# Second layer of a two-layer trunk: attention output projection by token halves, with the split weights of six units kept for the second half

## The chip, the cores and the metric

The kernel runs on one core of a Trainium2 chip. The metric is the time of one execution on the device in microseconds (us); the median of several runs counts.

## The reference

512 latent tokens and 256 context tokens of width 1024 pass two layers, each a token mixer and a squared-ReLU MLP. Every sub-layer sits between two RMS norms, modulated by a conditioning vector. The second layer's mixer is a neighbourhood attention; only its latent tokens are needed. After the attention this is what the second layer computes:

```python
def rmsnorm(t, g):
    tf = t.astype(jnp.float32)
    tf = tf * lax.rsqrt(jnp.mean(tf * tf, axis=-1, keepdims=True) + RMS_EPS)
    return tf.astype(t.dtype) * g

def sq_relu_mlp(h, w1, w2):
    return jnp.square(jax.nn.relu(h @ w1)) @ w2

def finish_layer(t, y, m, g, w1, w2):
    t = t + m[2] * rmsnorm(y, g[1])
    h2 = modulate(rmsnorm(t, g[2]), m[3], m[4])
    return t + m[5] * rmsnorm(sq_relu_mlp(h2, w1, w2), g[3])
...
            y = neighbourhood_attention(h, kc, vc, na_w_qkv[j], na_rpb[j]) @ na_w_out[j]
...
        x = finish_layer(x, y, m_lat, g, mlp_w1[i], mlp_w2[i])
```

`na_w_out` is 1024 x 1024, `w1` 1024 x 4096, `w2` 4096 x 1024, all in float32.

## The kernel before

Channels lie on the 128 partitions in eight blocks (`KB`), tokens along the free dimension: 512 latent tokens (`LAT`), for the first layer 256 context tokens more. The products are made in three passes of a reduced format: each operand is split into a high part (a copy in that format) and a low part (the rest), and high x high, high x low and low x high are added up in PSUM.

Weights come as units of 128 x 1024 (all eight input blocks for one block of 128 output channels). `Units.next` (L132) takes a unit that `wload` (L105) has loaded into one of two `raw` buffers (every third one into a third buffer, `raw2`), and `wsplit` (L114) splits it: ScalarE (ACT) writes the high part `wh` (L119), VectorE (DVE) the low part `wl` (L120), into two tiles each that take turns. TensorE (PE) then makes 24 matmuls per unit and column range, in `mm3` (L144).

The second layer's part after the attention is this. ACT copies the last attention result of a head pair out of PSUM (L1141), DVE adds the two halves (L1142, L1143); after all pairs each block is split into high and low (L1213, L1214). The output projection (L1235 to L1243) takes eight units against all 512 tokens, in two accumulators that take turns. After each unit `sums.add` (L295) works on the result: ACT squares it (L299) and scales it into the residual branch (L389), which frees the accumulator, DVE multiplies it by the stream x (L305), ACT squares the scaled one (L306), and GpSimd (POOL) adds the three products to running sums (L309). After the last unit `sums.factors` (L311) makes the norm factors of a token: PE adds the sums over the partitions (row sums, L263), DVE and ACT work out a reciprocal root (L321, L246 to L250), PE spreads it over the partitions again (L274) and ACT copies it (L275); the factors of the next norm (L334 to L338) follow in the same way. `join` (L361) goes over the eight blocks: multiply by the factor and add to x (`add_block`, L351 and L352: blocks 2, 4, 6 on POOL, the others on DVE), then split the modulated result into high (ACT, L377) and low (DVE, L378). This feeds the MLP (`mlp`, L884): four chunks, of each eight hidden units (`hidden`, L902) and then the product with `w2` (L954), added up by DVE (L960). The first two hidden units are begun together, block by block, as the blocks come out of the join; the list `early` says over which tokens, in which order. The last chunk's product (`c == 3`) goes by halves of 256 tokens (`HALVES`); each half loads and splits the eight units. After each half `after1` makes the factors of the last norm, adds and stores.

The order on each engine is made at build time by a scheduler from the program's order; `wsplit` runs under a higher priority (L117), so that splits are placed early on ACT and DVE. An engine works its list strictly in that order.

## Time and profile before

| what | us |
|---|---|
| median of 3 runs | 2187.4 |
| lowest, highest run | 2185.53, 2195.42 |
| profiled execution | 2191.73 |
| its span | 2189.9 |
| PE busy | 2073.0 (95% of the span) |
| DVE, ACT, POOL busy | 1278.6 (58%), 1008.4 (46%), 514.3 (23%) |
| mean granted clock of PE | 0.975 |

The profiled execution took 4.3 us more than the median. Times in the trace count from the start of the span. A PE row's duration includes its pipeline, so that the distance of two starts (the pitch) tells what a matmul costs. The granted clock is a share of 2.4 GHz.

### The profile page before, as it was taken

Reading aid. Unit: us, or ns where it says so; the run is one execution under the profiler, and the core shown is the slowest. Engines: PE = TensorE matmul, PEld = TensorE weight load, DVE = VectorE, ACT = ScalarE, POOL = GpSimd, SP = SyncE. Lnnn points to the kernel's source line nnn. Section 1 sums busy time; section 2 is a strip of 40 time slices with the busy share of each in tenths; the row PEclk is TensorE's granted clock in tenths of the full one; section 3 lists DMA queues with packets and bytes.
Section 4 is the critical chain, followed back from the end, with each engine's and each line's share of the span. In section 5 each row is a group of like instructions: output and inputs, shape, how many; then the busy total and the mean of one; then the engine's idle time right before and its main releaser. Section 6 shows DMA issues by size and latency. Waiting matters only on the chain.

```text
span 2189.9 us, 32496 instructions
## 1 busy us (share of the span) xinstructions
PE 2073.0 (95%) x12848; PEld 1733.5 (79%) x12848; DVE 1278.6 (58%) x2023; ACT 1008.4 (46%) x1751; POOL 514.3 (23%) x486
## 2 busy tenths in 40 slices
PE   6999998999999888999999999889999989999996
PEld 3777876878878766888888888668898768889895
DVE  5657968576683687314334244488777664345356
ACT  4565756567473553213223133356556643323244
POOL 0004435254451462000000001633222260000004
PEclk8999999999999999999999999989999989999998
DMA  6446758357676422333333111321111114222233
GB/s 253 135 152 187 234 158 238 115 173 221 192 200 235 156 74 85 107 114 116 116 116 114 59 59 68 106 78 50 56 54 54 49 50 155 95 97 87 97 107 115
DMA packets 93868, 269.72 MB, mean 123 GB/s; under 512 B 13074, under 2 KB 21652, under 8 KB 93716
## 3 DMA queue, kind: packets, MB, share of 16 engines
q1 hardware_dynamic: 85268, 242.47, 34.0%
q0 software_dynamic: 8448, 25.18, 4.4%
q8 instruction: 101, 1.65, 0.3%
q14 instruction: 51, 0.42, 0.1%
HBM read 244.27 MB, written 23.33 MB: 122 GB/s over the span
## 4 chain that ended last, share of the span: by engine, by line
PE 79%; DVE 9%; ACT 4%; DMA 3%; issue 2%; POOL 2%; SPq 0%; DVEq 0%; ACTq 0%; POOLq 0%
PE acc L902 21%; PE acc L144 21%; PE acc L954 20%; PE a L1048 4%; DMA E<-crow 2%; PE s L169 2%; PE a L1059 2%; PE yp L1134 1%; PE s L629 1%; DVE wl L120 1%; PE s L708 1%; PE pt L1119 1%; PE s L724 1%; PE s L263 1%; ACT wh L119 1%
## 5 line engine op out<-in xcount | busy, mean ns | idle before, releaser
L119 ACT ACTIVATE wh<-raw 128x1024 fp32r<-128x1024 f32 (+1 forms) x241 | 254.2, 1055 | 686.7 <-PE acc L954 309.7
L120 DVE TENSOR_TENSOR wl<-raw,wh 128x1024 fp32r<-128x1024 f32 (+1 forms) x241 | 301.9, 1253 | 255.1 <-ACT wh L119 248.6
L144 PE MATMUL acc<-hh,wh 128*128 128x512 f32 (+1 forms) x976 | 286.2, 370 | 7.8 <-ACT wh L119 3.0
L144 PE MATMUL acc<-hl,wh 128*128 128x512 f32 (+1 forms) x976 | 264.1, 346 | 0.5 <-DVE hl L762 0.5
L144 PE MATMUL acc<-hh,wl 128*128 128x512 f32 (+1 forms) x976 | 262.6, 344 | 2.0 <-DVE wl L120 2.0
L902 PE MATMUL acc<-hh,wh 128*128 128x258 f32 (+2 forms) x1024 | 242.8, 317 | 9.5 <-ACT hh L377 9.5
L954 PE MATMUL acc<-ah,wh 128*128 128x512 f32 (+1 forms) x832 | 247.4, 347 | 4.1 <-DVE ya L960 4.0
L902 PE MATMUL acc<-hl,wh 128*128 128x258 f32 (+2 forms) x1024 | 241.8, 314 | 3.9 <-DVE hl L378 3.8
L954 PE MATMUL acc<-ah,wl 128*128 128x512 f32 (+1 forms) x832 | 244.5, 343 | 0.8 <-DVE wl L120 0.8
L954 PE MATMUL acc<-al,wh 128*128 128x512 f32 (+1 forms) x832 | 244.8, 344 | 0.0
L902 PE MATMUL acc<-hh,wl 128*128 128x258 f32 (+2 forms) x1024 | 240.8, 313 | 0.0
L144 PEld LDWEIGHTS acc<-hh,wh 128*128 128x128 f32 (+1 forms) x976 | 155.2, 190 | 60.9 <-issue 38.3
L902 PEld LDWEIGHTS acc<-hh,wh 128*128 128x128 f32 x1024 | 160.9, 191 | 33.5 <-issue 11.5
L309 POOL TENSOR_TENSOR syy<-syy,last 128x512 f32<-128x512 f32 (+2 forms) x24 | 38.3, 1596 | 585.6 <-ACT last L299 585.5
L144 PEld LDWEIGHTS acc<-hh,wl 128*128 128x128 f32 (+1 forms) x976 | 153.7, 190 | 27.5 <-DVE wl L120 2.5
L902 PEld LDWEIGHTS acc<-hl,wh 128*128 128x128 f32 x1024 | 161.2, 191 | 17.9 <-DVE hl L378 5.9
L144 PEld LDWEIGHTS acc<-hl,wh 128*128 128x128 f32 (+1 forms) x976 | 154.2, 190 | 25.3 <-DVE hl L762 1.1
L902 PEld LDWEIGHTS acc<-hh,wl 128*128 128x128 f32 x1024 | 161.8, 191 | 11.6 <-DVE wl L120 0.4
L954 PEld LDWEIGHTS acc<-ah,wh 128*128 128x128 f32 x832 | 139.4, 189 | 32.7 <-issue 13.1
L954 PEld LDWEIGHTS acc<-ah,wl 128*128 128x128 f32 x832 | 139.6, 189 | 21.9 <-DVE wl L120 1.0
L954 PEld LDWEIGHTS acc<-al,wh 128*128 128x128 f32 x832 | 139.5, 189 | 20.0
L960 DVE TENSOR_TENSOR ya<-ya,acc 128x768 f32<-128x768 f32 (+2 forms) x56 | 40.6, 726 | 196.1 <-PE acc L954 196.1
(320 smaller groups left out, 3813.0 us busy)
## 6 DMA issues: line engine op xcount, KB each, us to landing
raw<-in_w_dram SPq DMA_DIRECT2D x136, 512.0 KB, 3.4
mraw<-in_modw_dram SPq DMA_DIRECT2D x72, 512.0 KB, 3.3
raw<-in_win_dram SPq DMA_DIRECT2D x48, 512.0 KB, 4.0
E<-crow SPq DMA_DIRECT2D x96, 256.0 KB, 5.0
eb<-erow POOLq DMA_DIRECT2D x96, 128.0 KB, 5.5
raw<-in_wout_dram SPq DMA_DIRECT2D x24, 512.0 KB, 3.7
raw<-in_modw_dram SPq DMA_DIRECT2D x8, 1024.0 KB, 17.8
raw<-in_wqk_dram SPq DMA_DIRECT2D x16, 512.0 KB, 3.3
```

The lines of the kernel that those rows point to most:

```text
L119: act.activation(wh[:, :n], raw[:, :n], AF.Copy)
L120: dve.tensor_tensor(wl[:, :n], raw[:, :n], wh[:, :n].bitcast(F32), ALU.subtract)
L144: pe.matmul(acc[:m, s0:s1], lhsT=ww[:, i * m:(i + 1) * m], rhs=xx[:, k, s0:s1], start=first and i == 0 and j == 0, stop=last and i == len( ...
L169: mm = pe.matmul(ps[32 * j:32 * j + 32, hf * 256:hf * 256 + 256], lhsT=cact[:, 8 * kg + 2 * j:8 * kg + 2 * j + 32], rhs=raw[:, j * 256:j * ...
L263: pe.matmul(ps[32 * j:32 * j + 32], lhsT=ones[:, :32], rhs=t[i], start=i == 0, stop=i == len(t) - 1)
L309: pool.tensor_tensor(t[:, s0:s1], t[:, s0:s1], d, ALU.add)
L629: pe.matmul(ps, lhsT=btok[:, d, c], rhs=xw.rearrange("p e q -> p (e q)"), start=True, stop=True)
L902: pe.matmul(acc[:, d0:d0 + s1 - s0], lhsT=ww[wi], rhs=xx[:, k, s0:s1], start=k == 0 and j == 0, stop=k == KB - 1 and j == 2)
L954: pe.matmul(acc[:, s0:s1], lhsT=ww[:, k * P:(k + 1) * P], rhs=xx[:, s0:s1], start=k == 0 and j == 0, stop=k == KB - 1 and j == 2)
L960: dve.tensor_tensor(y, y, acc[:, p0:p1], ALU.add)
L1048: pe.matmul(acc[:, :s1 - s0], lhsT=ws[ww][:, k * P:(k + 1) * P], rhs=xx[:, k, s0:s1], start=k == 0 and j == 0, stop=k == KB - 1 and j == 2)
L1059: pe.matmul(acc, lhsT=xx[:, k, i * P:(i + 1) * P], rhs=w[ww][:, sl], start=k == 0 and n == 0, stop=k == KB - 1 and n == 2)
```

## The change

In the second layer the projection now runs over the two token halves one after the other. In the first half the units 2 to 7 are split into tiles of their own (12 of 128 x 1024, in a pool that is opened when the attention's pool is closed and takes its place), and the second half uses them again; units 0 and 1 are loaded and split again. Norm factors and `join` come after each half. The MLP's first two units take the first half's tokens for all blocks, and then those of the second. In the last pass of the MLP's product, the units 2 to 7 are split in the first half into `hh` and `hl`, which nothing needs any more, and are used again in the second: six loads and six splits fewer.

```diff
--- before.py
+++ after.py
@@ -112,7 +112,16 @@
         sp.dma_start(raw[:, :src.shape[-1]], src)
         return raw
 
-    def wsplit(raw, n=1024):
+    def wsplit(raw, n=1024, into=None):
+        if into:
+
+            wh, wl = into
+            if len(wh.shape) == 3:
+                raw = raw.rearrange("p (k c) -> p k c", k=KB)
+            with tc.high_priority():
+                act.activation(wh, raw, AF.Copy)
+                dve.tensor_tensor(wl, raw, wh.bitcast(F32), ALU.subtract)
+            return into
         wh = wpool.tile([P, 1024], F32R, tag="wh", name="wh", bufs=2)
         wl = wpool.tile([P, 1024], F32R, tag="wl", name="wl", bufs=2)
         with tc.high_priority():
@@ -129,11 +138,11 @@
         def prefetch(self):
             self.ahead.append(wload(self.src[self.n + len(self.ahead)]))
 
-        def next(self):
+        def next(self, into=None):
             if not self.ahead:
                 self.prefetch()
             self.n += 1
-            return wsplit(self.ahead.pop(0))
+            return wsplit(self.ahead.pop(0), into=into)
 
     def mm3(acc, w, xh, xl, segs, first=True, last=True, m=P, ks=range(KB)):
         wh, wl = w
@@ -942,16 +951,23 @@
                     next(pieces, None)
                 for i, part in enumerate(passes if c == 3 else [(0, n)]):
                     w2.n = c * KB
+                    keep = c == 3 and len(passes) == 2 and l == 1
                     segs = [(max(part[0], s0), min(part[1], s1)) for s0, s1 in seg if s0 < part[1] and s1 > part[0]]
                     p0, p1 = part
                     for o in range(KB):
                         acc = acc_tile()
-                        wh, wl = w2.next()
+
+                        into = [q[:, :, (o - 2) * P:(o - 1) * P] for q in (hh, hl)] if keep and o > 1 else None
+                        if into and i:
+                            ww_ = into
+                        else:
+                            ww_ = [q if len(q.shape) == 3 else q.rearrange("p (k c) -> p k c", k=KB) for q in w2.next(into)]
+                        wh, wl = ww_
                         for k in range(KB):
                             ah, al = hid[k]
                             for j, (ww, xx) in enumerate(((wh, ah), (wh, al), (wl, ah))):
                                 for s0, s1 in segs:
-                                    pe.matmul(acc[:, s0:s1], lhsT=ww[:, k * P:(k + 1) * P], rhs=xx[:, s0:s1],
+                                    pe.matmul(acc[:, s0:s1], lhsT=ww[:, k], rhs=xx[:, s0:s1],
                                               start=k == 0 and j == 0, stop=k == KB - 1 and j == 2)
                         y = res[:, o, p0:p1]
                         if c == 0:
@@ -1232,15 +1248,22 @@
     A6 = scaled("A6", 1, 2, 4, True)
     hh, hl = yh, yl
     shift_cols(1, 3, LAT, hh, hl)
-    for p0, p1 in SEG[:1]:
-        wno = Units(a["wno"])
-        for o in range(KB):
-            acc = acc_tile()
-            mm3(acc, wno.next(), yh, yl, [(p0, p1)])
-            sums.add(o, acc, y1, x2, G5, p0, p1)
-        sl = slice(p0, p1)
-        sums.factors((0, 1))
-        join(y1, x2, sums, sl, A6, 0, hh, hl)
+
+    wno = Units(a["wno"])
+    with tc.tile_pool(name="wr", bufs=1) as wr:
+        parts = []
+        for n, (p0, p1) in enumerate(HALVES):
+            for o in range(KB):
+                acc = acc_tile()
+                if n == 0 and o > 1:
+                    parts.append(wno.next([wr.tile([P, 1024], F32R, name=f"w{q}{o}") for q in "hl"]))
+                elif n and o == 0:
+                    wno.n = 0
+                mm3(acc, parts[o - 2] if o > 1 else wno.next(), yh, yl, [(p0, p1)])
+                sums.add(o, acc, y1, x2, G5, p0, p1)
+            sl = slice(p0, p1)
+            sums.factors((n,))
+            join(y1, x2, sums, sl, A6, 0, hh, hl)
 
 
     G7 = [None]
@@ -1259,7 +1282,7 @@
                 sp.dma_start(out[:, ks, sl], x2[:, ks, sl])
 
     segs1 = [(0, 256, 0), (256, LAT + 2, LAT)]
-    mlp(1, SEG[:1], segs1, [segs1], HALVES, [(1, 10), (1, 11)], hh, hl, y1, x2, G7, between1, after1)
+    mlp(1, SEG[:1], segs1, [segs1[:1], segs1[1:]], HALVES, [(1, 10), (1, 11)], hh, hl, y1, x2, G7, between1, after1)
 
 
 # ---- launch: one core ----
```

Lines of the changed kernel: L122 and L123 are the kept splits, L128 and L129 the others; L308 and L398 square and scale (L299 and L389 before), L315 is the second square (L306); L1157 the copy (L1141), L1158 and L1159 the additions (L1142, L1143), L1229 and L1230 the splits of a block (L1213, L1214); L272, L386, L946 and L948 are L263, L377, L937 and L939.

On ACT at the end of the attention, before (the three `ph` are the attention's weights of the last head pair, `ya` with `hh` is block 7, `wh` belongs to unit 2, `syy` is the square of unit 0):

```order
L1120 ACTIVATE ph<-pt 128x512 x3
L1141 ACTIVATE ssqy<-yp 64x512
L1213 ACTIVATE hh<-ya 128x512
L119 ACTIVATE wh<-raw 128x1024
L299 ACTIVATE syy<-acc 128x512
L389 ACTIVATE ya<-acc,G_14924 128x512
```

and now:

```order
L1136 ACTIVATE ph<-pt 128x512 x3
L122 ACTIVATE wh_15043<-raw 128x1024
L122 ACTIVATE wh_15081<-raw 128x1024
L122 ACTIVATE wh_15119<-raw_15121 128x1024
L1157 ACTIVATE ssqy<-yp 64x512
L1229 ACTIVATE hh<-ya 128x512
L122 ACTIVATE wh_15157<-raw 128x1024
L122 ACTIVATE wh_15195<-raw 128x1024
L308 ACTIVATE syy<-acc 128x256
L398 ACTIVATE ya<-acc,G_14924 128x256
```

Five kept splits (units 2 to 6) now stand around the last copy and the last high part, three of them ahead of both. On PE the last attention matmul and what follows it is now:

```order
L1150 MATMUL yp<-ph,v 128x512
L153 MATMUL acc<-hh,wh 128x256 x2
L153 MATMUL acc<-hl,wh 128x256
L153 MATMUL acc<-hh,wl 128x256
L153 MATMUL acc<-hl,wh 128x256
L153 MATMUL acc<-hh,wl 128x256
L153 MATMUL acc<-hh,wh_15043 128x256
L153 MATMUL acc<-hl,wh_15043 128x256
```

Behind the last `yp` six matmuls of units 0 and 1 are left, all on block 7 of the tokens; then comes unit 2 with the kept weights. On DVE the three low parts stand in the same way ahead of the two additions and of block 7's low part, which before had no split ahead of them there.

On ACT between the halves of the projection (`s` is the spread factor, the `128x256` squares and scalings are those of units 0 and 1 of the second half) it is now:

```order
L308 ACTIVATE syy<-acc 128x256
L386 ACTIVATE hh<-xa,A_14961 128x256
L398 ACTIVATE ya<-acc,G_14924 128x256
L315 ACTIVATE ssqy<-ya 128x256
L255 ACTIVATE rt<-ms 32x256
L128 ACTIVATE wh<-raw 128x1024
L256 ACTIVATE rows<-rt 32x256
L386 ACTIVATE hh<-xa,A_14961 128x256 x4
L308 ACTIVATE last_14895<-acc 128x256
L398 ACTIVATE ya<-acc,G_14924 128x256
```

The four high parts of the first half's join stand ahead of the square and the scaling of unit 1; before, all high parts came behind all squares. PE has the six row sums of the first half (L272) directly behind its last matmul, and the second half's first matmul behind these.

On ACT at the start of the MLP's last pass, now:

```order
L128 ACTIVATE wh<-raw_18593 128x1024
L122 ACTIVATE hh<-raw 128x8x128 x2
L946 ACTIVATE last_6163<-last_6162,bt 128x512
L948 ACTIVATE ah<-last_6163 128x512
L122 ACTIVATE hh<-raw_18694 128x8x128
L122 ACTIVATE hh<-raw 128x8x128
L308 ACTIVATE syy<-ya 128x256
```

The kept splits of units 2 and 3 stand ahead of the work on the last hidden unit (L946, L948); before, only the splits into `wh` for units 0 and 1 did.

## Rows read from the trace of the kernel before

**Rows 1.** The page: PE's total (part 1), its weight loads (5), MLP weight loads (6).
```profile
PE 2073.0 (95%) x12848; PEld 1733.5 (79%) x12848; DVE 1278.6 (58%) x2023; ACT 1008.4 (46%) x1751; POOL 514.3 (23%) x486
...
L144 PEld LDWEIGHTS acc<-hh,wh 128*128 128x128 f32 (+1 forms) x976 | 155.2, 190 | 60.9 <-issue 38.3
...
raw<-in_w_dram SPq DMA_DIRECT2D x136, 512.0 KB, 3.4
```

**Rows 2.** Busy time in stretches: us long, each engine, clock, DMA share, GB/s.
```profile
1738.00:1772.00 34.00, 34.00 (x147) 27.19 (x145) 18.50 (x14) 17.51 (x26) 27.39 (x18) 1.00 0.34 109
1772.00:1783.00 11.00, 4.63 (x29) 1.87 (x28) 7.04 (x12) 4.24 (x8) 2.99 (x3) 0.79 0.14 48
1783.00:1799.00 16.00, 11.84 (x66) 9.83 (x66) 13.65 (x19) 6.17 (x12) 12.65 (x5) 0.82 0.00 0
1806.00:1850.00 44.00, 44.00 (x359) 39.64 (x358) 24.50 (x40) 17.03 (x23) 0.00 (x0) 1.00 0.55 178
728.00:752.00 24.00, 19.23 (x158) 18.05 (x157) 17.28 (x23) 19.46 (x32) 17.86 (x17) 1.00 0.45 151
```

**Rows 3.** The chain of waits, 1732 to 1812: start us, us, what.
```profile
1732.95 39.06 PE acc L144 x167
...
1780.70 0.02 POOLq L351
...
1804.90 0.57 PE s L169 x8
```

**Rows 4.** Timeline of PE, first layer's projection: start, us, engine line op [idle before].
```profile
742.15 0.28 PE L144 MATMUL acc<-yh,wh 128*128 128x256 f32 x1
...
743.51 0.28 PE L144 MATMUL acc<-yh,wh 128*128 128x256 f32 x1
```

**Rows 5.** Timelines of ACT and DVE at the end of the attention, 1732 to 1740.
```profile
1732.99 0.59 ACT L1141 ACTIVATE ssqy<-yp 64x512 f32<-64x512 f32 x1 [3.14 <-PE yp L1134]
...
1736.37 1.06 ACT L119 ACTIVATE wh<-raw 128x1024 fp32r<-128x1024 f32 x1 [1.32 <-PE acc L144]
...
1733.61 0.63 DVE L1142 TENSOR_TENSOR ya<-yp,ssqy 64x448 f32<-64x448 f32 x1 [2.90 <-ACT ssqy L1141]
...
1737.46 1.23 DVE L120 TENSOR_TENSOR wl<-raw,wh 128x1024 fp32r<-128x1024 f32 x1 [1.69 <-ACT wh L119]
```

**Rows 6.** Timelines of PE and ACT in the second layer's join.
```profile
1784.20 1.23 PE L902 MATMUL acc<-hh,wh 128*128 128x256 f32 x4 [4.22 <-ACT hh L377]
...
1786.54 0.63 PE L902 MATMUL acc<-hl,wh 128*128 128x256 f32 x2
...
1786.97 0.63 PE L902 MATMUL acc<-hh,wl 128*128 128x256 f32 x2
...
1790.74 0.36 ACT L275 ACTIVATE sxy<-s 128x256 f32<-128x256 f32 x1
```

**Rows 7.** Timelines of PE, POOL and DVE, first layer's row sums and 256-column join.
```profile
751.93 0.62 PE L263 MATMUL s<-syy,ones 128*32 128x256 f32 x2 [1.75 <-POOL syy L309]
...
766.02 0.74 POOL L351 TENSOR_TENSOR ya<-ya,syy 128x256 f32<-128x256 f32 x1 [11.59 <-ACT syy L275]
...
770.36 0.81 POOL L352 TENSOR_TENSOR xa<-xa,ya 128x256 f32<-128x256 f32 x1
...
775.13 1.37 DVE L352 TENSOR_TENSOR xa<-xa,ya 128x256 f32<-128x256 f32 x1
...
776.98 0.42 DVE L351 TENSOR_TENSOR ya<-ya,syy 128x256 f32<-128x256 f32 x1
...
777.88 0.48 DVE L378 SCALAR_TENSOR_TENSOR hl<-xa,A,hh 128x256 fp32r<-128x256 f32 x1
```

**Rows 8.** Timelines of PE and DVE in the last pass, between its halves.
```profile
2157.66 0.55 PE L954 MATMUL acc<-ah,wh 128*128 128x256 f32 x1 [3.99 <-DVE ya L960]
...
2154.44 1.74 DVE L120 TENSOR_TENSOR wl<-raw,wh 128x1024 fp32r<-128x1024 f32 x1
```

**Rows 9.** Timeline of POOL in the second layer's join.
```profile
1782.60 6.87 POOL L352 TENSOR_TENSOR xa<-xa,ya 128x512 f32<-128x512 f32 x1
```

## The prediction

> **What bounds the kernel now.** I read the page first. TensorE (PE) is busy 95% of the span [rows 1]: a change pays only where PE stands idle or at half clock. So I looked, stretch by stretch, at the parts that the diff touches [rows 2]. In the projection (1738 to 1772) PE has no gap: 34.00 of 34.00 us at clock 1.00. From 1772 to 1783 it is busy for 4.63 of 11 us at 0.79, from 1783 to 1799 for 11.84 of 16 at 0.82, and then it is dense again. This bubble is what the change aims at. Its chain of waits runs over the row sums, the factor arithmetic, the spreading and `join`. The projection's part starts at 1732.95 and lasts 39.06; the first two MLP units are done where the chain goes over to the next product at 1804.90 [rows 3]. So 32.9 us go by for 96 first-layer matmuls (two units), which take 44.00/359 = 0.123 us each in the dense stretch [rows 2] and 11.8 us in all; some 21 us are bubble.
>
> **The sum, part by part.** I start at 1732.96, where the last attention matmul ends, and keep to the profiled run: 2191.73 us, 4.3 above the median of 2187.4. Its difference is then put on the median.
>
> *Halving alone: nothing.* A matmul of 256 columns has a pitch of 0.1133 us (twelve from 742.15 to 743.51, [rows 4]). The new order has 42 of the 384 before the last attention matmul, so 342 x 0.1133 = 38.75 us remain, against 39.06 before [rows 3].
>
> *Attention's end: +9.4.* Before, ScalarE (ACT) copies the last attention result at 1732.99 (0.59), and DVE's two additions follow at 1733.61 [rows 5]; then ACT makes the last high part, block 7, while PE works on units 0 and 1 without a gap. In the new order three kept splits (units 2, 3, 4) stand ahead of that copy on ACT, and their three low parts ahead of the two additions on DVE. The kept tiles lie where the attention's tiles were, so these splits wait for the last attention matmul too. ACT: 1732.96 + 3 x 1.06 [rows 5] + 0.59 = 1736.7. DVE: the third low part begins near 1736.5 and takes 1.23 [rows 5]; the first addition takes 0.63, and for the second, with 64 columns instead of 448, I estimate a third of it: 1738.6. The high part, estimated at the copy's 0.59, is then there at 1739.2. Only six matmuls remain that need block 7 alone, all other work of units 0 and 1 having gone ahead: PE idles for 6.2 us. Then the splits of units 5 and 6 stand ahead of the square and the scaling that free unit 0's accumulator. Unit 6 reuses the buffer that unit 3's low part leaves at 1736.5; with 3.4 us for the load [rows 1] and 1.06 it ends near 1741.4, and the two ACT operations (0.36 each, as at 256 columns in [rows 6]) let unit 2 start at 1742.2: 1.7 more. After an idle of 4.22 us pairs came every 0.43 us (1786.54 to 1786.97, [rows 6]) instead of 2 x 0.123: about the lower clock level, 1.2 GHz; the stretch has 0.82 in the mean [rows 2]. Three us of it lose 1.5. Together 9.4. Ends: 5, if loads and splits are ready sooner and the clock holds; 12, if the last loads are late.
>
> *Sharing, both halves: +3.8.* The sums now run in twice as many, half as long operations. The nearest stretch is the first layer's own projection at 256 columns: from 728 to 752 PE was busy 19.23 of 24 us while GpSimd (POOL) was busy for 17.86 [rows 2], so a unit took some 3.26 us instead of 2.72. There every unit is split and read from memory; here six of eight aren't in the second half. For 14 units I take half of the difference, 14 x 0.27; the ends are 0 and 7.6.
>
> *Row sums of half 0: +3.0.* All six stand on PE ahead of any matmul of half 1, with their sums behind POOL's last additions. In the first layer such a wait was 1.75 us [rows 7]; six row sums of two matmuls cost some 1.3 us themselves. Ends 1.3 and 4.
>
> *Join of half 0 inside half 1: +2.5.* On ACT the high parts of blocks 1 to 4 stand ahead of the square of unit 1, which frees the accumulator of unit 3. They need POOL's blocks 2 and 4 and DVE's 1 and 3. POOL alone needs 0.87 us per operation (766.02 to 770.36 for five, [rows 7]): then nothing waits. In the first layer a DVE addition of the same join came as late as 775.13, 9 us after POOL's start [rows 7]; then PE waits 4. I take 2.5 between 0 and 4.
>
> The projection thus ends at 1732.96 + 9.4 + 38.75 + 3.8 + 3.0 + 2.5 = 1790.4, against 1772.0.
>
> *The end of half 1 and its join: 19 instead of 32.9.* Before, 8.7 us passed from the last matmul's end to the start of `join` (1780.70 in [rows 3]). Six factor operations, one after another, remain (0.42, as DVE's others of 256 columns, [rows 7]); three ACT operations of half size and one spread fewer bring it to 6. Then `join` at 256 columns: DVE's ten block operations of 0.42 and eight low parts of 0.48 [rows 7], with some 2.5 us of arithmetic for the other factors, make 10.5 us, and 2 for turns behind POOL: 12.5. Last matmuls 0.6. Half 0 of the two first MLP units (48 matmuls, 6 us) fills only part of it. Units 0 and 1 are done at 1809.4 instead of 1804.9: +4.5. Ends 16 and 21.
>
> *Two loads more: nothing.* Units 0 and 1 are loaded and split again for half 1; at 3.4 us a load [rows 1] both arrive under half 0's 17 us of matmuls.
>
> *Last pass of the MLP: +0.4.* Six loads and six splits go. They were hidden under the matmuls (1.06 and 1.23 us [rows 5] under 24 x 0.1133 = 2.72 a unit) apart from one place in the second half, where PE idled 3.99 us for a DVE addition that stood behind a split of 1.74 us begun at 2154.44 [rows 8]; some 1.5 of it go. Against that, two kept splits on ACT and their low parts on DVE now stand ahead of the work on the last hidden unit, whose results the pass needs: 2 x 1.06 less some slack, +1.9. Ends -1.5 and +2.
>
> Sum: 4.5 + 0.4 = **+4.9**, or 2196.6 on the profiled run and **2192.3** on the median (+0.2%).
>
> **Rivals.**
> 1. *The cover works; faster.* The kept splits run early enough not to hold the copy (term 5), the halves share without loss (0), the join hides (0), row sums cost 1.3, and the end takes 16: 1732.96 + 5 + 38.75 + 1.3 + 16 = 1794.0, 10.9 less; with the last pass 12.4 less: 2175. For it speaks that 21 us of bubble stand there; against it the two orders on ACT, which are fixed.
> 2. *DVE and POOL take turns, and half 1 is bound by them; slower.* In the trace one waits for the other: a POOL operation of 512 columns, which at 0.87 per 256 should take 1.7, lasted 6.87 us while DVE was busy in the same join [rows 9]. If they exclude each other, half 1 needs POOL 24 x 0.87 = 20.9 and DVE 10.5 for the join, 8 x 0.41 for the products and 2.5 for two splits: 37 us, where the 21.8 of PE and my shares make 27. The projection ends 10 us later: +15, 2202. It decides as soon as the turns exceed PE's 21.8 us. Against it: in the projection before, POOL's 27.39 and DVE's 18.50 busy us of 34 [rows 2], which add to more than the stretch, left PE without a gap.
> 3. *The smaller matmuls pay for their weights.* A weight load is 190 ns in the trace [rows 1]. If it stood between matmuls, the 192 additional ones would cost 36 us: 2224. Against it stands the pitch of 0.1133 us with loads of other weights before each matmul [rows 4]. The Trainium skill (TensorE: Matmul & The Clock Gate, section "Measured speedup vs the span model") says that a weight load overlaps running matmuls only where the row group differs, which here it never does; by its load figure of 107 ns, the estimate is 20 us, or 2208. The trace disagrees: at 0.1133 us a 107 ns matmul leaves no room for such a load. Chance 1%.
> 4. *The kept weights do nothing.* Splits run on ACT and DVE beside a PE that never waited for them in the projection: then they can't bring more than the last pass's 1.5 us. That is part of my sum, not a case of its own.
>
> **How the numbers follow.** The forecast, within 0.5% (10.9 us, near the spread of the three runs shown, 2185.5 to 2195.4, and about what a measurement of this kernel can tell from no change): 0.54. Rival 1 and its neighbours, faster by over 0.5%: 0.18. Rival 2, slower by over 0.5%: 0.27; rival 3: 0.01, so slower has 0.28. All low ends together give 2175, all high ends (12, 7.6, 4, 4, 21, 2) 2205. These don't meet often, so the range is 2176 to 2204; it takes in most of rival 2.
>
> **What would show it.** In the changed profile: a PE idle of some 6 us after the last attention matmul, released by the high part of block 7; half clock behind it; unit 2 at about 9 us after that matmul; six row sums of half 0 with a wait before them; the projection's last matmul near 1790; the two MLP units near 1809; an addition in the last pass that waits less. The prediction is wrong if the gap at the attention's end is under 4 us, if the projection ends before 1782 or after 1796, or if the bubble behind it is under 5 us.

## The result, and the profile after

The changed kernel takes 2209.18 us in the median of four runs (2208.33 to 2210.95), the kernel before 2186.47 (four runs, 2185.38 to 2195.42). The medians differ by 22.7 us; the ratio of the runs is 1.0088, with a 95% interval of 1.0070 to 1.0106, or 15 to 23 us. The kernel is slower, and its time lies beyond the upper end of the range, 2204.0. The sign was that of the likeliest number (2192.3); the size was some four times too small.

Where the time lies is seen best from a point that both kernels share: the end of the last attention matmul (start and duration of the last row of `yp`), called **the mark** below. In the kernel before it lies at 1732.96 and the span ends at 2189.9, 456.9 us later. In the changed kernel it lies at 1732.22, and the span ends 476.9 us later, 19.9 more. The whole difference of the two spans, 19.2 us, thus lies behind the mark. From the mark to the end, the kernel before and then the changed one, and behind them the stretches of the changed kernel that answer to [rows 2] (us long, PE, its weight loads, DVE, ACT, POOL, clock, DMA share, GB/s):

```profile
1732.96:2189.90 456.94, 426.29 (x2780) 378.50 (x2779) 231.06 (x313) 169.58 (x234) 69.11 (x48) 0.97 0.30 101
...
1732.22:2209.10 476.88, 441.77 (x2954) 396.45 (x2954) 235.66 (x347) 173.31 (x266) 60.83 (x72) 0.96 0.29 92
...
1732.00:1742.00 10.00, 2.27 (x8) 1.54 (x7) 6.95 (x8) 6.97 (x10) 0.00 (x0) 0.74 0.47 167
1742.00:1762.00 20.00, 20.00 (x146) 19.66 (x147) 9.50 (x11) 10.20 (x24) 14.20 (x18) 0.87 0.42 129
1762.00:1797.00 35.00, 30.22 (x210) 26.82 (x209) 23.84 (x40) 16.94 (x42) 21.06 (x24) 0.90 0.10 31
...
1804.00:1824.00 20.00, 16.10 (x77) 11.82 (x77) 13.09 (x27) 6.00 (x13) 5.00 (x6) 0.74 0.08 26
```

Of the 19.9 us only 4.5 are idle time of PE (35.1 us instead of 30.7); 15.5 are time in which it is busy. The stretch from 1732, the attention's end, has PE busy for 2.27 of 10 us, where it had no gap. The one from 1762, the second half's projection, has 30.22 of 35 us at 0.90 and should have no gap either. The one from 1804 is what is left of the bubble: 16.10 of 20 us at 0.74. These rows of PE's timeline show the gaps and what ended them:

```profile
1738.40 0.80 PE L153 MATMUL acc<-hh,wh 128*128 128x256 f32 x2 [6.19 <-ACT hh L1229]
...
1741.89 0.58 PE L153 MATMUL acc<-hh,wh 128*128 128x256 f32 x1 [1.54 <-ACT ya L398]
...
1742.27 0.41 PE L153 MATMUL acc<-hl,wh 128*128 128x256 f32 x1
...
1742.48 0.41 PE L153 MATMUL acc<-hh,wl 128*128 128x256 f32 x1
...
1751.09 0.28 PE L153 MATMUL acc<-hh,wh 128*128 128x256 f32 x1
...
1751.20 0.28 PE L153 MATMUL acc<-hl,wh 128*128 128x256 f32 x1
...
1761.55 0.62 PE L272 MATMUL s<-syy,ones 128*32 128x256 f32 x2
...
1764.26 0.39 PE L153 MATMUL acc<-hh,wh 128*128 128x256 f32 x1
...
1777.23 0.39 PE L153 MATMUL acc<-hh,wh 128*128 128x256 f32 x1 [3.12 <-ACT ya L398]
...
1780.08 1.22 PE L283 MATMUL s<-rows,sel 32*128 32x256 f32 x2 [1.66 <-DVE rows L259]
```

After the mark PE idles for 6.19 us until block 7's high part is there, and for 1.54 until the first accumulator is free. Behind that the matmuls come every 0.21 us (1742.27 to 1742.48), later every 0.12. The row sums of half 0 start at 1761.55, and the second half at 1764.26, without a wait. In the second half there are two gaps, 3.12 us for the scaling of unit 1 and 1.66 us for the next norm's factors, and behind them the matmuls come every 0.21 us again, until 1784.6. On ACT and DVE the same places read:

```profile
1732.30 2.95 ACT L122 ACTIVATE wh<-raw 128x1024 fp32r<-128x1024 f32 x3 [3.11 <-PE yp L1150]
...
1735.27 0.59 ACT L1157 ACTIVATE ssqy<-yp 64x512 f32<-64x512 f32 x1
...
1737.72 0.63 ACT L1229 ACTIVATE hh<-ya 128x512 fp32r<-128x512 f32 x1 [1.86 <-DVE ya L1159]
...
1733.39 3.50 DVE L123 TENSOR_TENSOR wl<-raw,wh 128x1024 fp32r<-128x1024 f32 x3 [3.22 <-ACT wh L122]
...
1736.91 0.63 DVE L1158 TENSOR_TENSOR ya<-yp,ssqy 64x448 f32<-64x448 f32 x1
...
1774.78 1.77 ACT L386 ACTIVATE hh<-xa,A 128x256 fp32r<-128x256 f32 x4 [1.36 <-DVE xa L361]
...
1776.46 0.36 ACT L308 ACTIVATE last<-acc 128x256 f32<-128x256 f32 x1
...
1769.09 0.95 DVE L361 TENSOR_TENSOR xa<-xa,ya 128x256 f32<-128x256 f32 x1
```

Three kept splits (2.95 us) run before the copy at 1735.27, and three low parts (3.50 us) before the addition at 1736.91; in the second half four high parts (1.77 us) before unit 1's square at 1776.46. The rest is the second join and the two MLP units behind it:

```profile
1796.51 0.62 PE L272 MATMUL s<-syy,ones 128*32 128x256 f32 x2
...
1805.12 0.42 DVE L360 TENSOR_TENSOR ya<-ya,syy 128x256 f32<-128x256 f32 x1 [0.78 <-ACT syy L284]
...
1806.45 0.84 DVE L361 TENSOR_TENSOR xa<-xa,ya 128x256 f32<-128x256 f32 x1
...
1813.32 0.41 DVE L259 SCALAR_TENSOR_TENSOR rows<-rt,rows 32x256 f32<-32x256 f32 x1
...
1817.42 1.27 DVE L387 SCALAR_TENSOR_TENSOR hl<-xa,A,hh 128x256 fp32r<-128x256 f32 x3
...
1806.22 0.79 POOL L361 TENSOR_TENSOR xa<-xa,ya 128x256 f32<-128x256 f32 x1
...
1810.74 0.39 PE L911 MATMUL acc<-hl,wh 128*128 128x258 f32 x1 [2.35 <-DVE hl L387]
...
1814.61 1.22 PE L283 MATMUL s<-rows,sel 32*128 32x256 f32 x2
...
1816.27 1.06 PE L178 MATMUL s<-mraw,cact 128*32 128x256 f32 x2
...
1817.99 1.08 PE L178 MATMUL s<-mraw,cact 128*32 128x256 f32 x6
...
1819.59 0.42 PE L911 MATMUL acc<-hl,wh 128*128 128x258 f32 x1
1819.81 0.42 PE L911 MATMUL acc<-hh,wl 128*128 128x258 f32 x1
...
1823.74 0.28 PE L911 MATMUL acc<-hh,wl 128*128 128x258 f32 x1
```

The second half's projection ends at 1796.5, its join begins on DVE at 1805.12 and ends at 1818.69, and the two units end only at 1823.9, one pitch behind the start of their last matmul (in the kernel before at 1804.9, the last step of [rows 3]). DVE's additions take 0.84 us while POOL is busy in its own, instead of 0.42. DVE has the next norm's factors at 1813.7, and PE spreads them at 1814.61. Of the second half's 48 matmuls 31 stand behind this spreading, and eight matmuls of the modulation (L178) are put in between, from 1816.27 on. PE doesn't wait there; it works at half pace, one matmul in 0.22 us (1819.59 to 1819.81).

In the last pass the sum of the terms came as forecast, the two parts of it larger. The row sums of its two halves lie here in the kernel before and after:

```profile
2142.91 0.62 PE L263 MATMUL s<-syy,ones 128*32 128x256 f32 x2 [0.17 <-POOL syy L303]
...
2172.88 0.62 PE L263 MATMUL s<-syy,ones 128*32 128x256 f32 x2
```

```profile
2165.41 0.62 PE L272 MATMUL s<-syy,ones 128*32 128x256 f32 x2
...
2178.00 0.38 PE L970 MATMUL acc<-ah,hh 128*128 128x256 f32 x1 [1.80 <-DVE ya L976]
...
2192.43 0.62 PE L272 MATMUL s<-syy,ones 128*32 128x256 f32 x2
```

From the mark to the first it is 409.95 us before and 433.19 after, 23.2 more; to the second 439.92 and 460.21, 20.3 more. The first half of the pass lost some 3 us, and the second gave 2.9 back: its gap is 1.80 us instead of 3.99 [rows 8].

### The profile page after: what moved, and what is told of

Read it like the earlier page. It is cut to its first block, busy times and chain, and to the rows that moved or that the text cites. A ratio compares the mean times of both kernels' runs of the same rounds, so it can differ in the third digit from the quotient of the medians.

```text
span 2209.1 us, 32950 instructions
## 1 busy us (share of the span) xinstructions
PE 2090.6 (95%) x13040; PEld 1752.6 (79%) x13040; DVE 1281.8 (58%) x2057; ACT 1011.9 (46%) x1783; POOL 505.6 (23%) x510
## 4 chain that ended last, share of the span: by engine, by line
PE 77%; DVE 10%; DMA 4%; issue 4%; ACT 3%; POOL 2%; SPq 0%; DVEq 0%; ACTq 0%; POOLq 0%
PE acc L911 21%; PE acc L970 20%; PE acc L153 18%; PE a L1064 4%; DMA E<-crow 2%; PE s L178 2%; PE a L1075 2%; PE yp L1150 1%; PE s L638 1%; DVE wl L129 1%; PE s L272 1%; PE s L717 1%; PE pt L1135 1%; PE s L733 1%; DVE xa L361 1%
## 5 line engine op out<-in xcount | busy, mean ns | idle before, releaser
L128 ACT ACTIVATE wh<-raw 128x1024 fp32r<-128x1024 f32 (+1 forms) x225 | 237.1, 1055 | 659.6 <-PE acc L970 295.7
L129 DVE TENSOR_TENSOR wl<-raw,wh 128x1024 fp32r<-128x1024 f32 (+1 forms) x225 | 281.5, 1251 | 234.6 <-ACT wh L128 218.6
L153 PE MATMUL acc<-hh,wh 128*128 128x256 f32 (+3 forms) x1040 | 300.4, 360 | 17.4 <-ACT hh L1229 6.2
L153 PE MATMUL acc<-hh,wl 128*128 128x256 f32 (+3 forms) x1040 | 276.3, 336 | 2.0 <-DVE wl L129 2.0
L153 PE MATMUL acc<-hl,wh 128*128 128x256 f32 (+3 forms) x1040 | 277.4, 337 | 0.5 <-DVE hl L771 0.5
L970 PE MATMUL acc<-ah,wh 128*128 128x512 f32 (+1 forms) x736 | 219.9, 355 | 0.8 <-ACT ah L948 0.8
L970 PE MATMUL acc<-al,wh 128*128 128x512 f32 (+1 forms) x736 | 218.0, 352 | 0.2 <-DVE al L949 0.2
L970 PE MATMUL acc<-ah,wl 128*128 128x512 f32 (+1 forms) x736 | 217.4, 351 | 0.0
L318 POOL TENSOR_TENSOR syy<-syy,last 128x256 f32<-128x256 f32 (+2 forms) x30 | 36.6, 1221 | 593.6 <-ACT last L308 593.6
L970 PEld LDWEIGHTS acc<-ah,wh 128*128 128x128 f32 x736 | 120.7, 188 | 29.0 <-issue 8.7
L970 PEld LDWEIGHTS acc<-al,wh 128*128 128x128 f32 x736 | 120.8, 188 | 20.7 <-DVE al L949 0.4
```

The source lines that it names most:

```text
L128: act.activation(wh[:, :n], raw[:, :n], AF.Copy)
L129: dve.tensor_tensor(wl[:, :n], raw[:, :n], wh[:, :n].bitcast(F32), ALU.subtract)
L153: pe.matmul(acc[:m, s0:s1], lhsT=ww[:, i * m:(i + 1) * m], rhs=xx[:, k, s0:s1], start=first and i == 0 and j == 0, stop=last and i == len( ...
L318: pool.tensor_tensor(t[:, s0:s1], t[:, s0:s1], d, ALU.add)
L970: pe.matmul(acc[:, s0:s1], lhsT=ww[:, k], rhs=xx[:, s0:s1], start=k == 0 and j == 0, stop=k == KB - 1 and j == 2)
```

## The experiments

The runs were made on five chips, each beside the kernel before on the same one, whose medians there were 2192.2 to 2194.0. Executions of the same kernel reach the mark at different times (1732.22 and 1736.36 in two profiles of the changed kernel), but what follows the mark repeated in these two: 476.88 and 476.94 us to the span's end. So the table sets the ratio of the times beside what each profile shows from the mark. "Row sums 1" is the start of those of the second half, "units" the end of the first two MLP units, one pitch behind the start of their last matmul (a dash where the order of their matmuls makes it another thing).

| run | ratio to before, interval | mark | span | mark to row sums 1 | mark to units | mark to end |
|---|---|---|---|---|---|---|
| before | 1 | 1732.96 | 2189.9 | (39.2) | 71.9 | 456.9 |
| changed | 1.0088, 1.0070 to 1.0106 | 1732.22 | 2209.1 | 64.3 | 91.6 | 476.9 |
| a2_after | 1.0094, 1.0075 to 1.0114 | 1736.36 | 2213.3 | 64.3 | 91.5 | 476.9 |
| e1_late_splits | 1.0068, 1.0053 to 1.0083 | 1734.70 | 2208.3 | 60.5 | 88.2 | 473.6 |
| e2_no_w2_keep | 1.0084, 1.0069 to 1.0099 | 1730.80 | 2207.7 | 64.5 | 91.9 | 476.9 |
| e3_no_early | 1.0083, 1.0066 to 1.0100 | 1729.19 | 2204.6 | 64.7 | - | 475.4 |
| e4_no_wno_keep | 1.0094, 1.0072 to 1.0116 | 1731.31 | 2211.6 | 68.9 | 96.3 | 480.3 |
| e5_r_late | 1.0089, 1.0074 to 1.0104 | 1736.29 | 2210.8 | 61.5 | 82.4 | 474.5 |
| e9_combined2 | 1.0045, 1.0029 to 1.0060 | 1732.71 | 2200.5 | 56.5 | 77.4 | 467.8 |
| e10_no_pool | 1.0078, 1.0058 to 1.0097 | 1737.00 | 2212.0 | 60.2 | 86.8 | 475.0 |
| e11_before_r_mid | 1.0002, 0.9987 to 1.0017 | 1736.90 | 2193.9 | (39.2) | - | 457.0 |
| e12_before_stride | 0.9996, 0.9984 to 1.0008 | 1735.67 | 2192.3 | (39.2) | - | 456.6 |
| e13_best | 1.0080, 1.0064 to 1.0095 | 1742.07 | 2211.1 | 58.0 | 78.9 | 469.0 |
| e14_after_stride | 1.0077, 1.0057 to 1.0097 | 1730.95 | 2208.0 | 64.4 | 91.9 | 477.1 |
| e15_warm | 1.0100, 1.0079 to 1.0121 | 1732.94 | 2212.0 | 64.9 | 94.2 | 479.1 |
| e16_combined_warm | 1.0043, 1.0019 to 1.0068 | 1729.77 | 2197.1 | 56.0 | 82.5 | 467.3 |
| e17_before_warm | 0.9994, 0.9978 to 1.0009 | 1730.57 | 2187.6 | (39.2) | - | 457.0 |
| e18_combined_no_pool | 1.0028, 1.0015 to 1.0041 | 1733.07 | 2199.3 | 54.9 | 76.2 | 466.2 |
| e19_all_waits | 1.0033, 1.0019 to 1.0047 | 1738.12 | 2203.0 | 54.0 | 75.1 | 464.9 |
| e20_splits_behind | 1.0059, 1.0038 to 1.0080 | 1736.17 | 2209.9 | 61.1 | 88.5 | 473.7 |

In brackets stands the kernel before's one set of row sums.

**The attention's end.** First the kept splits lost their high priority:

```diff
-            with tc.high_priority():
+            with tc.high_priority() if len(wh.shape) == 3 else nullcontext():
                 act.activation(wh, raw, AF.Copy)
```

> The change with the kept splits of the projection at normal priority, so that the copy of the last attention result stands ahead of them on ACT. Theory A (what the kept splits hold up at the attention's end is lost for good): PE's idle there falls from 7.7 us to 1 to 3, the half clock behind it goes, and the time falls by 5 to 9 us, to 2200 to 2204. Rival B (half 1 and its join are bound by DVE and POOL taking turns, not by when they start): the gap closes, but the time falls by under 2 us, 2207 or more.

It brought 3.3 us to the end, less than theory A said and more than rival B. The copy now came first, but two splits still stood ahead of block 7's high part. So they were then put behind block 7's parts on both engines:

```diff
-                    parts.append(wno.next([wr.tile([P, 1024], F32R, name=f"w{q}{o}") for q in "hl"]))
+                    with tc.issue_after(t7), tc.issue_after(t8):
+                        parts.append(wno.next([wr.tile([P, 1024], F32R, name=f"w{q}{o}") for q in "hl"]))
```

> The change with one thing alone: the kept splits of the projection stand behind block 7's high and low part, on ACT and on DVE. Theory A: the gap of 6.2 us falls to the 2 us of the copy and the additions, another short one stays for the first accumulator, the row sums of half 0 start 4.5 to 6.5 us sooner after the attention's last matmul, and the time from there to the end falls by as much, to 471 to 473 us. Rival (a later wait takes it up): the row sums start sooner, but the end comes less than 2 us sooner.

The timelines of PE and ACT in this run:

```profile
1738.31 0.50 PE L153 MATMUL acc<-hh,wh 128*128 128x256 f32 x2 [2.14 <-ACT hh L1229]
...
1738.16 2.94 ACT L122 ACTIVATE wh<-raw 128x1024 fp32r<-128x1024 f32 x3
...
1741.78 0.58 PE L153 MATMUL acc<-hh,wh 128*128 128x256 f32 x1 [2.00 <-ACT ya L398]
```

The gap of 6.19 us is 2.14, with 0.23 behind it, but the wait for the accumulator grew from 1.54 to 2.00: the end comes 3.2 us sooner, not 4.5 to 6.5. Of the idle time that stays, 2.4 us are the copy and the additions. In the kernel before, PE still had matmuls of units 0 and 1 left at this place; in halves those are 42 short ones, all spent before the mark. The 2.00 us are still the splits': three of them (2.94 us from 1738.16) stand on ACT between block 7 and the scaling that frees the accumulator. With normal priority, where one stands there, that wait was 0.41 us, but two stood ahead of block 7 and its gap was 3.23.

The other way, without kept tiles at all:

```diff
-                if n == 0 and o > 1:
-                    parts.append(wno.next([wr.tile([P, 1024], F32R, name=f"w{q}{o}") for q in "hl"]))
-                elif n and o == 0:
+                if n and o == 0:
                     wno.n = 0
-                mm3(acc, parts[o - 2] if o > 1 else wno.next(), yh, yl, [(p0, p1)])
+                mm3(acc, wno.next(), yh, yl, [(p0, p1)])
```

> The change with nothing kept in the projection: each half loads and splits all eight units into the two alternating buffers. Theory A (the kept splits' place is what costs at the attention's end): no gap of 6 us there, 6 to 9 us less than the changed kernel, 1.004 to 1.006 times before. Rival E (keeping relieves DVE and ACT in half 1 by as much): the gap at the attention's end goes, but half 1 gets longer by 4 us or more, and the time stays within 3 us of the changed kernel.

Rival E holds. The gap of 6.19 us is 2.14 here too, but the second half gets longer, with 2.46 us of PE waiting for a low part and 2.35 for POOL:

```profile
1795.01 0.39 PE L153 MATMUL acc<-hh,wl 128*128 128x256 f32 x1 [2.46 <-DVE wl L129]
...
1800.24 0.62 PE L272 MATMUL s<-syy,ones 128*32 128x256 f32 x2 [2.35 <-POOL syy L318]
```

From the mark to the second row sums it is 68.9 us instead of 64.3, and to the end 3.4 more. By these two profiles keeping the weights is worth that much once the projection is halved, in spite of where the splits stand; the times of the two kernels, 1.0094 both, can't tell them apart.

**The last pass.** `keep` was set to False.

> The change without the kept weights in the MLP's last pass. Theory A: what the first half loses (3.5 us) the second gives back (2.9 us), so the time stays within 1.5 us of 2209. Rival C (the kept splits ahead of the last hidden unit cost more than they save): 2206 or less. If the saved splits matter: 2212 or more.

476.9 us from the mark to the end, as with it: neither a gain nor a loss. Its first row sums of the last pass start 430.0 us after the mark, 3.2 sooner, and the second at 460.1, as with the kept weights: the kept splits cost 3.2 us ahead of the pass and save 3.1 in it.

**The first two MLP units.** `[segs1[:1], segs1[1:]]` went back to `[segs1]`.

> The change with the first two MLP units taken block by block over both halves, as before. Theory A (the matmuls of half 0 fill the wait for the row sums of half 1): that wait is empty again and the 96 matmuls follow the join, so 2 to 6 us more, 2211 to 2215. Rival D (PE is at half clock behind the join whatever it does first): within 1.5 us of 2209.

1.5 us less from the mark, against theory A: taking half 0 first costs a little. Its matmuls stand between the row sums of half 1, and the first spreading behind those came 6.4 us after the first of them here, 7.5 with the change.

**The next norm's factors.** They were worked out for both halves together, behind the second join:

```diff
-            sums.factors((n,))
-            join(y1, x2, sums, sl, A6, 0, hh, hl)
+            on = sums.factors((n,), later=True, on=on)
+            join(y1, x2, sums, sl, A6, 0, hh, hl)
+        sums.second((0, 1), *on)
```

> The change with the factors of the next norm worked out for both halves together and after the second join, since only the end of a hidden unit needs them. Theory A (waits in order): PE's wait of 1.66 us in half 1 goes with the spreading matmuls at half clock behind it, and six DVE operations leave each join, which took 0.42 to 0.85 us each: 5 to 9 us less, 2200 to 2204. Rival B (turns with POOL bind the join): POOL's operations still hold DVE, under 3 us less, 2206 or more.

The units were done 82.4 us after the mark instead of 91.6, 9.2 sooner, more than either theory said. Of the 27.3 us between the second row sums and the units, 20.9 are left: the join's last low part comes 18.6 us after the row sums instead of 22.2, and the units end 2.2 us behind it instead of 5.1. The modulation matmuls now stand behind the units too, and most of the matmuls run at the full pace. Another 2.8 came in the second half, where PE's wait for these factors is gone. But most of the gain was given back at once, since the units' end needs the factors, and two high-priority splits now stood ahead of them on ACT and DVE:

```profile
1815.13 1.27 DVE L394 SCALAR_TENSOR_TENSOR hl<-xa,A,hh 128x256 fp32r<-128x256 f32 x3
...
1819.05 2.36 DVE L129 TENSOR_TENSOR wl<-raw,wh 128x1024 fp32r<-128x1024 f32 x2
...
1822.22 0.42 DVE L259 SCALAR_TENSOR_TENSOR rows<-rt,rows 64x256 f32<-64x256 f32 x1
...
1822.69 0.71 PE L283 MATMUL s<-rows,sel 32*128 32x256 f32 x4 [3.94 <-DVE rows L259]
```

PE waits 3.94 us, and only 2.4 us reach the end.

**All three waits.** Kept splits at normal priority, the first join traced behind unit 1 of the second half, and the next norm's factors traced between blocks 4 and 5 of the second join:

```diff
+            if mid and k == 5:
+                mid()
...
+                if n and o == 1:
+                    join(y1, x2, sums, slice(*HALVES[0]), A6, 0, hh, hl)
```

> The change with all three waits in order taken away at once: kept splits of the projection at normal priority, the first half's join traced behind unit 1 of the second half, the next norm's factors for both halves together, traced between blocks 4 and 5 of the second join. Theory A (the waits add up): 3.5 at the attention's end, 5 in half 1, 8 in the second join, 14 to 17 us less than the changed kernel, about 1.002 times before. Rival B (DVE and POOL in turns, and a PE at half clock, bind the second join whatever comes before): under 8 us less, 1.005 or more.

9.1 us from the mark to the end, and 1.0045 times before against 1.0094 of the changed kernel on that chip: less than theory A said, and somewhat more than rival B. PE's timeline shows what is left:

```profile
1776.09 0.39 PE L153 MATMUL acc<-hh,wh 128*128 128x256 f32 x1 [2.88 <-ACT ya L407]
...
1814.12 0.58 PE L920 MATMUL acc<-hh,wh 128*128 128x256 f32 x2 [2.68 <-DVE last L953]
```

The wait in the second half is still there, though the join was moved; it ends with the same scaling. And behind the units, which end 77.4 us after the mark, PE waits 2.68 us for their last step, which needs the next norm's factors.

The changed kernel as it is ran beside this one:

> The changed kernel as it is, again, beside the others on one chip, so that their differences don't hang on the chip. All theories: 1.007 to 1.011 times the kernel before, with the same gaps.

It agrees with the first measurement, gap by gap.

**DVE and POOL.** The two joins were taken off POOL (`join` with an empty set of POOL's blocks):

> The change with all blocks of its two joins on DVE and none on POOL. Rival B (DVE and POOL exclude each other in the join, DVE's operations take 0.84 us there instead of 0.42): DVE gains six or seven times 0.42 and takes six more of 0.42, so the second join stays as long within 1 us; if POOL's own blocks are what PE waits for, it gets shorter by 3 us or more. Theory A (order of the waits): the join in half 1 and its wait of 3.1 us change by under 1.5 us, the time stays within 2 us of the changed kernel (1.0085 to 1.0105 times before).

In the second half the wait of 3.12 us is gone, and DVE's first additions of the first join take 0.41 where they took 0.95:

```profile
1772.63 0.41 DVE L361 TENSOR_TENSOR xa<-xa,ya 128x256 f32<-128x256 f32 x1
...
1797.18 0.62 PE L272 MATMUL s<-syy,ones 128*32 128x256 f32 x2 [2.06 <-POOL syy L318]
```

So that wait was not ACT's order alone, as theory A said; ACT stood there because the blocks came late, and they came late by DVE's and POOL's work on them side by side. Of the 6.2 us by which the projection ends sooner, POOL's additions, which pile up behind, take 2.06 back. The second join with its units stays as long (26.7 us), as rival B said. Up to the first row sums of the last pass this run is 3.4 us ahead of the changed kernel (429.8 us from the mark instead of 433.2). Of this 1.5 us go in the last pass, where behind the same gap of 1.80 us the matmuls came at half pace for 3.2 us, which they did in no other run with this gap; so the end is only 1.9 us sooner. With the first join alone on DVE, in the kernel without the three waits:

> The kernel with all three waits taken away, and the blocks of the first join all on DVE. Rival B (DVE's turns with POOL are what the wait of 2.9 us in half 1 still consists of): that wait goes and the second row sums start 2 to 5 us sooner; from the attention's last matmul to the end 463 to 466 us instead of 467.8. Theory A (the wait was ACT's order alone): within 1 us.

The wait of 2.88 us falls to 0.54, and 1.6 us come through to the end, less than rival B said and more than theory A. With the kept splits behind block 7's parts as well:

> The same, and the kept splits behind block 7's parts on both engines. If the terms add up: 2 to 3 us less than that, 460 to 464 us from the attention's last matmul to the end, 1.001 to 1.003 times before; the change then costs 4 to 7 us with no wait in order left.

464.9 us from the mark, 1.3 less, where 2 to 3 were expected; by their times (1.0028 and 1.0033) the two runs can't be told apart. The sum stays 7.9 us above the kernel before. Nor are all waits gone: two splits still stand ahead of the first scaling (0.76 us), and the 2.68 us behind the units are there too. No version with halves came below the kernel before.

**The clock.** 56 matmuls of the kind

```diff
+                                    pe.matmul(accs[0][:, 256:512], lhsT=ws[0][0][:, :P], rhs=hh[:, 0, :256], start=True, stop=True)
```

were put ahead of the second half's blocks.

> The changed kernel with 56 matmuls on an unused piece of an accumulator, ahead of the blocks of the second half in the first two MLP units: they compute nothing that is used, and keep PE busy where it waits for the second join. Theory H (the last matmuls of these units come 5 us behind the join's last low part because PE idled and its clock was granted at half): the pitch behind the gap is 0.12 instead of 0.21, and the units are done 2 to 4 us sooner after the attention's last matmul (88 to 89.5 us instead of 91.5). Rival I (PE is late there by the order of its work, the modulation matmuls among it, not by its clock): done later than 91 us.

The run doesn't decide it. The matmuls did not keep the clock up:

```profile
1812.00:1818.00 6.00, 5.34 (x24) 4.26 (x25) 5.55 (x15) 2.99 (x7) 0.00 (x0) 0.63 0.00 0
1818.00:1824.00 6.00, 6.00 (x43) 6.00 (x43) 1.17 (x3) 0.51 (x1) 0.00 (x0) 0.80 0.00 0
```

It was granted at 0.63 and 0.80 in the mean, and the units were done 2.6 us later. Some 36 of the added matmuls stood behind the spreading of the factors and made work of their own there, and the modulation matmuls stand behind the units in this run. How much of the lag is the clock stays open here.

> The kernel with all three waits taken away, and the same 56 matmuls. Theory H: no more than 1 us either way, since there the units were done 1 us behind the join already and the last factors are waited for; 1.0045 times before again.

467.3 us against 467.8: no difference, as expected, though the units end 82.5 us after the mark instead of 77.4. In that kernel the end of the units is not what the rest waits for.

> The kernel before with 60 such matmuls between its row sums and its join. Theory: its join is paced by DVE and POOL, so the clock alone gives 0 to 2 us; within 2 us of before. If PE's half clock paced it: 3 us less or more.

In the kernel before, PE's gap of 4.22 us [rows 6] shrinks to 0.68, and the clock was 1.00 up to 1783, but the end is where it was:

```profile
1782.04 0.75 PE L902 MATMUL acc<-hh,wh 128*128 128x256 f32 x4 [0.68 <-ACT hh L377]
...
1785.77 0.80 PE L902 MATMUL acc<-hl,wh 128*128 128x256 f32 x2 [2.98 <-DVE hl L378]
```

Filling the first gap thus gains next to nothing, as the theory said: the join on DVE and POOL paces the bubble. The clock in the join itself isn't tried by it, since behind the wait of 2.98 us it was granted at 0.50 until 1790. Up to the first row sums of the last pass the run is 1.1 us ahead (408.9 us instead of 410.0), which went in the last pass at a lower clock (0.51 for 5.8 us behind the gap of 3.99 us, 0.71 in the kernel before).

**Three tries that moved nothing or the wrong thing.** The factors alone, moved in the kernel before:

> The kernel before, with only the next norm's factors moved between blocks 4 and 5 of its join. If these DVE operations (six of 0.4 to 1.5 us among the first blocks) delay the join: 2 to 4 us less than before. If the join there is bound by POOL's blocks: within 1 us of before.

457.0 us: nothing. Rows of 768 elements instead of 770, in the kernel before and in the changed one (`h_tiles(T)` in place of `T + 2` columns):

> The kernel before with rows of 768 instead of 770 elements per block in the second layer's split tokens. Theory F (a matmul of 256 columns takes 0.119 us where an operand lies in the tile with rows of 770 elements, 0.114 where none does): the 1536 first-layer matmuls of the MLP take 0.114 and the time falls by 5 to 8 us. Rival G (the pitch hangs on something else in these stages): the pitch stays at 0.119 and the time within 1.5 us of before.

> The changed kernel with rows of 768 elements in the second layer's split tokens. Theory F: projection, first MLP product and the last pass with kept weights (some 2100 matmuls of 256 columns) take 0.114 us instead of 0.119, 8 to 11 us less than the changed kernel, 1.005 to 1.006 times before. Rival G: within 2 us of the changed kernel.

Nothing either; the pitch stayed at 0.12 us, and theory F falls. All of it together, with the attention's blocks at high priority:

> The change with the waits in order taken away as in the run with all three, the high parts of the attention's blocks at high priority, the first join one unit later in half 1, and rows of 768 elements. Theory A with F: 3 us more at the attention's end and in half 1, and 8 to 10 us by the pitch: 0.996 to 0.999 times before. Rival B: not below 1.002.

It is no better: 469.0 us from the mark, and the wait in the second half grew to 4.09 us with the join one unit later. The mark itself lies at 1742.07, later than in any other profile, so the high priority of the blocks seems to have made the attention longer. One profile can't show that, but the times point the same way: 1.0080 against 1.0045 for the run with all three, with intervals apart, where the mark to the end differs by 1.2 us only.

## Why the prediction was wrong, point by point

**Attention's end: right in mechanism, too small by 2 us.** Forecast were a gap of 6.2 us for block 7 and 1.7 for the accumulator; they are 6.19 and 1.54. The matmuls at half clock, from 1741.89 on, lasted for some 24 of them, at 0.213 instead of 0.119: 2.3 us, where I had 1.5 for all, and the six of block 7 before them took 1.95 us instead of 0.7. (In the working of the second gap 1736.5 + 3.4 + 1.06 is 1741.0, not 1741.4.)

**Halving alone: nothing; that failed, by 2 us.** The pitch here is 0.119 us, not 0.1133 of the first layer: 342 x 0.0057.

**Sharing, 3.8: wrong in the first half, where it cost nothing.** 144 matmuls from 1741.89 to 1761.55 took 19.7 us; at 0.119 they are 17.1, and the half clock is the rest. POOL kept up with the matmuls. (The unit taken as 3.26 us should have been 2.72 x 24 / 19.23 = 3.39.)

**Row sums of half 0: right.** 3.0 were forecast, and 1761.55 to 1764.26 is 2.7, though without a wait for POOL.

**Join of half 0 inside half 1, 2.5: too small.** The second half took 32.25 us (1764.26 to 1796.51), and its 192 matmuls at 0.119 are 22.8: 9.4 us more, where join and sharing together had 4.7 for it. It is the wait of 3.12 us for unit 1's scaling, the upper half of my bounds; 1.66 us for the next norm's factors, whose spreading I had overlooked on PE, where it stands in the middle of the second half's matmuls; the two spreadings themselves; and half clock from 1781 to 1784.6. The runs without POOL's blocks show what the first of these hangs on: DVE and POOL side by side in the join.

The projection thus ended 64.3 us after the mark instead of 57.4, at 1796.5, beyond the 1796 that the prediction had named as a sign of being wrong.

**The end of half 1 and its join, 19 instead of 32.9: this is the step that failed most.** It is 27.3 us (1796.5 to 1823.9). To the join's start it was 8.6 instead of 6. First-layer matmuls between the row sums on PE are 0.7 of this: without them it was 7.9. The join took 13.6 instead of 12.5. The "last matmuls 0.6" are 5.1: I let PE follow the join block by block, but the spreading of the next norm's factors and eight modulation matmuls stand in its list between the blocks, from 1814.6 to 1819.0, and 31 of the 48 matmuls are then still to do, most of them at half pace. With the factors moved the 27.3 fall to 20.9, 3.5 of it in the join and 2.9 in what follows it. I had counted their arithmetic as 2.5 us on DVE, and neither what they put into PE's list nor its half pace; the run does not part these two.

**Last pass: right in the sum, partly by luck.** +0.4 was forecast, and the run without kept weights there has the same end to 0.1 us. But both parts were larger than in the sum, 3.2 us lost instead of 1.9 and 3.1 saved instead of 1.5, and cancel.

**The rivals.** Rival 2 (the turns of DVE and POOL, 2202) named the right side and two thirds of the size, and the turns are there: 0.84 and 0.95 us where 0.41 is the time alone. But taking POOL out of the joins, which also gives DVE twelve more operations, gives 3.4 us up to the last pass and 1.9 to the end, so they were a part and not the bound. Rival 3 (weight loads between the short matmuls) fell with the pitch. By the rule of the Trainium skill (TensorE: Matmul & The Clock Gate, section "The mechanism", where the rule stands) each of the 256-column matmuls would have waited for a load of its own of some 107 ns, an estimate of 0.21 us a matmul; the trace has 0.119 at the upper clock, so that the rule doesn't hold for this stream of loads and matmuls. Rival 4's point held: the kept weights of the last pass do nothing.

**What is shown and what not.** Shown by runs: 3.2 us for the splits ahead of block 7; 6.4 us between second row sums and units, and 2.8 in the second half, for the place of the next norm's factors, of which 2.4 reach the end while the splits hold them up; 1.6 to 3.4 us for POOL's blocks; all of these together 12.0 us of the 19.9. The 7.9 us that stay are only read from the rows of that last run, here from the mark to its end:

```profile
1738.12:2203.00 464.88, 435.32 (x2954) 393.04 (x2954) 233.60 (x345) 171.37 (x264) 61.39 (x66) 0.97 0.29 95
```

PE is idle for 29.6 us, 1.1 less than before, and busy for 9.0 more. What stays is thus not waiting but longer work. Read in steps of 1 us, PE was busy at the lower clock level for 11.9 us in the kernel before, 25.5 in the changed one and 15.6 in the last run. If such work takes half as long at the upper level, the half clock is an estimated 6.8 us of the 19.9 and 1.9 of the 7.9. The pitch is an estimated 1.9 us in the projection and 1.5 in the kept units of the last pass, and half 0's row sums are 2.7; no run tries these apart.

## What to carry to other kernels

Splitting a stage in two to hide its closing chain under its second half pays for that chain twice, and each time in the lists of all engines: look for the closing chain's instructions on the busiest engine (here the spreadings on PE), and count everything that stands behind them there and what their arithmetic delays on the others, not their own time. Here work at high priority was placed ahead of the end of the stage whose memory it takes, and then waited for that end with the rest of the list behind it. To compare such versions, measure from a point that all of them share: here the medians of the kernel before differ by up to 7.5 us from one measurement to the next (2186.5 to 2194.0), and the time from the mark repeated to 0.1. Look at the clock even so: behind the same gap in the last pass it fell in one profile and not in the others, for 1.5 us.

## What the hardware showed that I had not expected

Matmuls of 256 columns at a granted clock of 1.00 have two pitches in these kernels: 0.113 to 0.114 in the first layer's projection and in the last pass of the kernel before, and 0.118 to 0.120 in the second layer's halved projection, in the MLP's first product of both kernels and in the last pass with kept weights. It looked like the tile with rows of 770 elements, but with 768 it stayed; the cause is open. After an idle of 6.19 us the matmuls came at half pace for over 5 us (1741.89 to 1747.1), and even 56 filling matmuls with a gap of 2.30 us among them left the clock at 0.63 for the next 6 us.
